# Seven channel-major products take both halves of x in one pass of 512 columns

## The chip, the cores and the metric

One core of a Trainium2 chip runs the whole kernel. The metric is the device time of one execution in microseconds, taken as the median of several runs. The engines work side by side and synchronise through semaphores: PE (TensorE) multiplies matrices, PEld is its weight load, DVE (VectorE) and ACT (ScalarE) do elementwise work and read PSUM, POOL (GpSimd) does a little, SP (SyncE) issues the DMAs.

## The reference

Two transformer-like blocks follow each other on 256 tokens of 1024 channels, all in float32.

```python
# block 1: S5 state-space branch and dilated attention
h = rms_norm(x, norm_w)
u_s, z_s, q, k, v, z_a, r_s, r_a = split(h @ w_in)
y_s = (s5_branch(u_s, ..., w_glu) * silu(z_s)) @ w_ssm_out     # s5: g * sigmoid(g @ w_glu)
y_a = (dilated_attention(q, k, v) * silu(z_a)) @ w_attn_out
x = x + (sigmoid(r_s) * y_s + sigmoid(r_a) * y_a) @ w_o
# block 2: HGRN2 branch, differential attention, mixture of experts
h = rms_norm_2(x, norm_mix)
hq, hf, hi, hog, dq, dk, dv, gate_hg, gate_da = split(h @ w_in_2)
o_hg = rms_norm_2(hgrn2(hq, 1 - f, hi, log(f))) * silu(hog)    # f from hf
mixed = sigmoid(gate_hg) * (o_hg @ w_branch_hg) + sigmoid(gate_da) * (o_da @ w_branch_da)
x = x + mixed @ w_out
x = x + hier_moe(rms_norm_2(x), ...)                           # top 2 of 8 experts in 1 of 4 groups
```

## The kernel before

**Products in three terms.** A float32 product is done in PE's fp32r format with both operands split into a rounded part (hi) and a remainder (lo). Each product is w_hi·x_hi + w_hi·x_lo + w_lo·x_hi, summed in PSUM. Weights arrive by DMA as float32 half-blocks of 128 partitions by 1024 values (512 KB) in buffers WR2 or WR3. ACT copies such a half-block to an fp32r buffer (the hi part, a copy of 128x1024 at line 272), DVE subtracts that from the original (the lo part, 128x1024 at line 253). Five fp32r buffers (one called WR0, two WR1, two WR4) rotate through these hi and lo parts. So the lo part of a half-block goes to the buffer that PE gives back when it ends the half-block two before it, and is needed when PE ends the one before it.

**The function `dense`** (line 438) computes 256 output channels by 256 tokens in one PSUM bank, called d (there are two of them). It takes two half-blocks of weights, one for each half of the 1024 input channels. Each half-block is 2 groups of 128 channels (j) by 4 slices of input channels (kk) by three terms: 24 matmuls of 256 columns at line 453, 48 for the block. Then `evac` reads the bank: DVE or ACT takes both j in one instruction of 128x512.

**What runs.** Block 1 ends with the gate rs (4 blocks), the product glu (4), the attention output ao (4, with smaller weights), the state-space output so (4) and the output product wo. Block 2 begins with hf and hq (2 blocks), then hi, hog (2), dq, dk, dv, the gates gh (4) and gd (4), the branch outputs bh and bd, and the last product wo2. hi, dq, dk, dv, wo and wo2 are token-major: `dense_wide` (line 467), matmuls of 512 columns at line 477, with other halves of the weights. `dense2` (line 489) does hf at line 502. The sequential parts (dilated attention, HGRN2, differential attention) are generators that give side work to PE between half-blocks (`side_run`); lines 935, 954 and 969 are the dilated attention's matmuls.

**Order.** The program's order is what the code issues, after a scheduler that moves an instruction of an engine ahead of others where it reckons that these would wait; each engine then runs its own list strictly in order. `prefetch` issues the loads of the mixture's weights at a rate per block, as far as there is free space. The mixture (lines 1995 and 2027) ends the kernel.

**PSUM.** Its eight banks are d (2 tiles of one bank), s (3 tiles of one bank), s2 (one tile of two banks) and o (one bank). s2 is used by the scan of HGRN2 and by a few steps of the first block. A tile has its readers and writers tracked as a whole where parts of it cannot be told apart.

Of the kernel before, what the change touches and what calls it, by code (L numbers as in the profile page):

```python
# [205 lines left out]
class Buf:  # L206
# [7 lines left out]
    def free(self):  # L214
        h = self.heap
        h.clock += 1
        for i in range(self.s, self.s + self.nu):
            assert h.used[i]
            h.used[i] = False
            h.freed[i] = h.clock  # L220


# [18 lines left out]
class Kernel:  # L241
# [196 lines left out]
    def dense(self, key, x_hi, x_lo, evac, token_major=False, k=8, rows_first=False):  # L438
# [26 lines left out]
        self.side_run()  # L465

    def dense_wide(self, key, x_hi, x_lo, evac):

# [124 lines left out]
    def tanh_half(self, out, ps):  # L593
        self.scaled(out, ps)
        self.act(out, out, AF.Tanh, scale=0.5)

# [436 lines left out]
    def setup(self):  # L1033
        nc, I = self.nc, self.I
        self.side, self.mid = [], []
        self.mheaps = [self.F]
# [18 lines left out]
    def first_block(self):  # L1055
# [132 lines left out]
        big = {n: F.alloc(3072, top=True) for n in "kqv"}  # L1188
        self.g_hi, self.g_lo = R.alloc(8, 256), R.alloc(8, 256)
        ssm = self.ssm(u2, u3)  # L1190
# [43 lines left out]
        def last(which, c):  # L1234

            if which == WHOLE[-1] and c == 5:
                hT.extend((R.alloc(8, 256), R.alloc(8, 256)))
                self.mid.extend(halves(i) for i in range(4))
# [5 lines left out]
        for which in ORDER[1:ORDER.index("so")]:  # L1244
# [24 lines left out]
            elif which in width:  # L1269
                g = gate[which] = F.alloc(width[which], 256)  # L1270
                for c in range(width[which] // 2):
                    self.dense(which, hT[0], hT[1], (silu2 if which[0] == "z" else tanh_half)(g, c))
# [38 lines left out]
            elif which == "glu":  # L1311
                zs = gate["zs"]
                s_hi, s_lo = R.alloc(8, 256), R.alloc(8, 256)
# [12 lines left out]
                self.g_hi.free()  # L1326
# [6 lines left out]
        for c in range(4):  # L1333
            def ev(ps, c=c):
                w = slice(2 * c, 2 * c + 2)
                self.stt(rs[:, w], rs[:, w], 1.0, ps, ALU.add, ALU.mult)
                t = self.E.alloc(2, 256)
                nat = t.ap.rearrange("p b (c s) -> p b s c", s=4)
                for b in range(2):
                    self.stt(nat[:, b], ra[:, 2 * c + b].rearrange("p (s c) -> p s c", s=4), 4.0,  # L1340
                             rs[:, 2 * c + b].rearrange("p (s c) -> p s c", s=4), ALU.mult, ALU.add)
# [6 lines left out]
        self.hT2 = R.alloc(8, 256), R.alloc(8, 256)  # L1348

# [272 lines left out]
    def second_block(self):  # L1622
# [44 lines left out]
        for c in range(2):  # L1667
            def ev(ps, c=c):
                self.scaled(hq[:, 2 * c:2 * c + 2], ps)
            self.dense("hq", hT[0], hT[1], ev)  # L1670
        hv = F.alloc(2, 512)
# [9 lines left out]
        for c in range(2):  # L1681
            def ev(ps, c=c):
                self.silu2(hog[:, 2 * c:2 * c + 2], ps)
            self.dense("hog", hT[0], hT[1], ev)
        self.side_add(hg, SIDE[3])
# [26 lines left out]
        for key in ("gh", "gd"):  # L1712
            gates[key] = F.alloc(8, 256)
            for c in range(4):
                def ev(ps, c=c, g=gates[key]):
                    self.tanh_half(g[:, 2 * c:2 * c + 2], ps)
                self.dense(key, hT[0], hT[1], ev)
        self.side_drain(hg)
        for b in hT + (self.rows,):
            b.free()  # L1720
# [525 lines left out]
def lay(inputs):  # L2246
# [22 lines left out]
    for name, blocks in (("w_in", (8, 10, 12, 20, 22, 24)), ("w_wo", (0, 2)), ("w_in_2", (4, 8, 10, 12)), ("w_wo2", (0,))):  # L2269
        for c in blocks:  # L2270
            two = A[name][c:c + 2]
            A[name][c:c + 2] = two.transpose(1, 2, 0, 3).reshape(two.shape)
    for name, key in (("w1", "w1_2"), ("w3", "w3_2"), ("w2", "w2_2")):
        w = f[key][0]
# [57 lines left out]
```

## Time and profile before

| | |
|---|---|
| median of 3 runs | 1035.3 us (1034.04 to 1035.33) |
| the profiled execution | 1034.89 us, of which the span from first to last instruction is 1033.1 us |
| mean granted TensorE clock | 0.975 |
| busy: PE, PEld, DVE, ACT | 926.3, 640.1, 518.6, 346.8 us |
| the chain that ended last, by engine | PE 53%, DMA 39%, DVE 6% |

The span is shown in 40 slices of 25.8 us on the page. Up to about slice 24 PE is busy nearly all the time, and from there the DMA engines are.

### The profile page before, as it was taken

The numbers are of one execution on the slowest core, as the hardware profiler recorded it, in microseconds if no ns is written. First come the engines' busy times: TensorE is split into PE (matmuls) and PEld (weight loads), VectorE is DVE, ScalarE is ACT, GpSimd is POOL, SyncE is SP. The second block draws the span as 40 slices with busy tenths as digits, with TensorE's granted clock in tenths as the row PEclk, the third lists the DMA queues.
The fourth block names the chain that finished last, engine by engine and source line by source line (L and its number), as shares of the span: only waits on it lengthen the run. The fifth ranks groups of instructions, "written<-read, shape, count | busy, mean of one in ns | idle before, by whom it ended". The sixth has DMA issues, their size and how long they took to land.

```text
span 1033.1 us, 17476 instructions
## 1 busy us (share of the span) xinstructions
PE 926.3 (90%) x7171; PEld 640.1 (62%) x7171; DVE 518.6 (50%) x1166; ACT 346.8 (34%) x574; POOL 13.4 (1%) x41
## 2 busy tenths in 40 slices
PE   8999999999999999999999999877868687787865
PEld 6887788998999988888999844321313122131312
DVE  8988987987767768596767521110101010010101
ACT  3227567455554457544644311000000000000000
POOL 2100000000000000000000000000000000000000
PEclk9999999999999999998999999998999998998989
DMA  7965655654437755652569899999999999999996
GB/s 258 223 192 170 173 159 163 191 185 164 160 128 238 238 197 172 194 182 87 182 200 331 339 394 419 421 423 420 421 421 421 421 422 421 421 420 423 421 417 264
DMA packets 65814, 296.91 MB, mean 287 GB/s; under 512 B 12224, under 2 KB 17728, under 8 KB 42176
## 3 DMA queue, kind: packets, MB, share of 16 engines
q1 hardware_dynamic: 65728, 295.73, 76.8%
q8 instruction: 58, 0.95, 0.4%
q14 instruction: 28, 0.23, 0.1%
HBM read 293.61 MB, written 2.10 MB: 286 GB/s over the span
## 4 chain that ended last, share of the span: by engine, by line
PE 53%; DMA 39%; DVE 6%; ACT 1%; issue 1%; SPq 0%; DVEq 0%; ACTq 0%
PE d L453 27%; DMA heap<-in_w_dram 25%; PE d L477 12%; DMA WR<-in_w_dram 12%; DVE heap L253 3%; DMA WR<-in_w_last_dram 2%; DVE WR L253 2%; PE h L1995 2%; PE s L935 1%; PE d L502 1%; ACT heap L272 1%; PE o L969 1%; PE s L954 1%; PE d L1817 1%; PE r L2027 1%
## 5 line engine op out<-in xcount | busy, mean ns | idle before, releaser
L453 PE MATMUL d<-R,WR 128*128 128x256 f32 x1920 | 240.3, 285 | 0.5 <-DVE WR L253 0.4
L453 PEld LDWEIGHTS d<-R,WR 128*128 128x128 f32 x1920 | 232.8, 192 | 5.5 <-issue 2.8
L1995 PE MATMUL h<-heap 128*32 128x512 f32 x1024 | 176.5, 667 | 61.8 <-DMA heap<-in_w_dram 60.7
L253 DVE TENSOR_TENSOR WR<-WR,WR 128x1024 fp32r<-128x1024 f32 x140 | 170.9, 1222 | 75.8 <-PE d L453 23.3
L272 ACT ACTIVATE WR<-WR 128x1024 fp32r<-128x1024 f32 x140 | 148.1, 1058 | 125.5 <-PE d L453 82.7
L1995 PEld LDWEIGHTS h<-heap 128*32 128x32 f32 x1024 | 40.0, 119 | 183.5 <-DMA heap<-in_w_dram 111.5
L477 PE MATMUL d<-WR,R 128*128 128x512 f32 x624 | 150.5, 398 | 2.9 <-ACT heap L272 1.5
L477 PEld LDWEIGHTS d<-WR,R 128*128 128x128 f32 x624 | 116.9, 190 | 29.5 <-DVE WR L253 2.2
L253 DVE TENSOR_TENSOR heap<-heap 128x512 f32<-128x512 f32 (+7 forms) x250 | 108.5, 483 | 1.8 <-PE s L785 0.7
L2027 PE MATMUL r<-WR,heap 128*32 128x512 f32 (+1 forms) x288 | 78.7, 550 | 10.3 <-DMA WR<-in_w_dram 9.3
L272 ACT ACTIVATE heap<-heap 128x512 f32<-128x512 f32 (+7 forms) x125 | 65.8, 539 | 65.2 <-DVE heap L253 29.3
L269 DVE SCALAR_TENSOR_TENSOR WR<-r,ring,WR 128x512 fp32r<-128x512 f32 (+1 forms) x18 | 12.4, 691 | 136.5 <-ACT WR L272 136.5
L2027 PE MATMUL r<-R,heap 128*32 128x512 f32 (+1 forms) x288 | 69.7, 551 | 9.4 <-ACT heap L272 4.8
L453 PE MATMUL d<-WR,WR 128*128 128x256 f32 x320 | 71.5, 382 | 2.2 <-DMA WR<-in_w_in_dram 2.2
L453 PEld LDWEIGHTS d<-WR,WR 128*128 128x128 f32 x320 | 60.1, 190 | 12.7 <-ACT R L272 3.7
L253 DVE TENSOR_TENSOR heap<-heap,h 128x512 f32<-128x512 f32 x8 | 5.5, 688 | 122.1 <-PE h L1995 122.0
L2027 PEld LDWEIGHTS r<-WR,heap 128*32 128x32 f32 x288 | 19.3, 109 | 56.7 <-DMA WR<-in_w_dram 26.8
L272 ACT ACTIVATE WR<-r,ring 128x512 fp32r<-128x512 f32 (+1 forms) x18 | 11.5, 640 | 125.0 <-PE r L2027 113.3
L272 ACT ACTIVATE heap<-h,ring 128x512 f32<-128x512 f32 x8 | 5.5, 687 | 134.5 <-PE h L1995 112.9
L269 DVE SCALAR_TENSOR_TENSOR heap<-heap,h 128x512 f32<-128x512 f32 x8 | 5.5, 688 | 83.5 <-ACT heap L272 83.4
L2027 PEld LDWEIGHTS r<-R,heap 128*32 128x32 f32 x288 | 14.8, 109 | 36.5 <-issue 15.5
L272 ACT ACTIVATE heap<-r 128x512 f32<-128x512 f32 x8 | 4.8, 597 | 80.3 <-PE r L2010 80.3
(215 smaller groups left out, 798.8 us busy)
## 6 DMA issues: line engine op xcount, KB each, us to landing
heap<-in_w_dram SPq DMA_DIRECT2D x128, 1024.0 KB, 19.8
WR<-in_w_in_dram SPq DMA_DIRECT2D x114, 512.0 KB, 3.8
R<-in_w_dram SPq DMA_DIRECT2D x28, 1024.0 KB, 19.8
WR<-in_w_dram SPq DMA_DIRECT2D x28, 1024.0 KB, 19.8
WR<-in_w_wo_dram SPq DMA_DIRECT2D x16, 512.0 KB, 5.6
WR<-in_w_glu_dram SPq DMA_DIRECT2D x8, 512.0 KB, 3.7
WR<-in_w_so_dram SPq DMA_DIRECT2D x8, 512.0 KB, 4.7
R<-in_w_last_dram SPq DMA_DIRECT2D x8, 512.0 KB, 12.6
```

Of the source, the lines that this page charges most:

```text
L253: (eng or self.V).tensor_tensor(out=out, in0=a, in1=b, op=op)
L269: self.V.scalar_tensor_tensor(out=out, in0=a, scalar=s, in1=b, op0=op0, op1=op1)
L272: self.A.activation(out, a, func, **kw)
L453: self.PE.matmul(ps[:, j], lhsT, rhs, start=h == 0 and i == 0 and n == 0, stop=h == k - 4 and kk == 3 and n == len(terms) - 1, skip_group_ ...
L477: self.PE.matmul(ps[tb], x[:, h + kk, sl], w[:, kk], start=h == 0 and kk == 0 and n == 0, stop=h == 6 and kk == 1 and n == 2)
L502: self.PE.matmul(ps[c][:, j], lhsT, rhs, start=h == 0 and i == 0 and n == 0, stop=h == 4 and kk == 3 and n == 2, skip_group_check=True)
L935: PE.matmul(ps[hh][:, cols], qT[r, q, qs], kT[r, q, k], start=True, stop=True)
L954: PE.transpose(pt[:, kb], s[:, kb * 128:(kb + 1) * 128], self.ident)
L969: PE.matmul(po[hp][r, qb], v[:, tb, g * 8 + hp * 2 + hh], ts_[hh][:, kb], start=kb == 0, stop=kb == 3)
L1817: PE.matmul(ps, x[:, 4 * h + kk, tb * 128:tb * 128 + 128], ws[h][w][:, kk], start=h == 0 and kk == 0 and n == 0, stop=h == 1 and kk == 3 a ...
L1995: PE.matmul(ph[sl[g]], xg[:, kk, sl[g]], w(name, kk // 4, g)[:, kk % 4], start=kk == 0, stop=kk == 7)
L2027: PE.matmul(pys[c][sl[g]], hT[:, kk, sl[g]], rhs, start=kk == 0, stop=kk == 3)
```

## The change

`dense_both` takes the place of `dense` for the seven products rs, glu, so, hq, hog, gh and gd: 24 blocks of 256 channels. x_hi and x_lo now lie beside each other in one buffer (R has two buffers of twice the size in place of four). The weights of these products are laid out on the host so that a half-block holds one j (128 channels) with all eight slices of input channels. For each slice one matmul of 512 columns takes w_hi against both halves of x, into the two halves of one PSUM bank, and one of 256 columns adds w_lo·x_hi to the first half: 16 matmuls per half-block in place of 24. At eviction ACT copies the second half of the bank to SBUF and DVE adds the first half (`total`), and what `evac` did on 128x512 it does on 128x256, once for each j. `turn` starts as True and is inverted before each block: the first block of a product takes its two banks as two tiles d, the second as the one tile s2, and so on in turn. Twelve of the 24 blocks take s2.

```diff
+    def dense_both(self, key, x_hi, x_lo, evac):
+        both = x_hi.both
+        self.turn = not self.turn
+        two = self.psum("s2", 2, 2, 256) if self.turn else None
+        for j in range(2):
+            ps = self.psum("d", 2, 256) if two is None else two[:, j]
+            hi, lo = self.next_weights(key)
+            w_hi, w_lo = (shaped(b.ap.rearrange("p a b -> p (a b)"), (8, 128)) for b in (hi, lo))
+            for kk in range(8):
+                self.PE.matmul(ps, w_hi[:, kk], both[:, :, kk], start=kk == 0, stop=False, skip_group_check=True)
+                self.PE.matmul(ps[:, 0], w_lo[:, kk], both[:, 0, kk], start=False, stop=kk == 7, skip_group_check=True)
+                if kk % 4 == 3:
+                    self.run_mid(1)
+            hi.free()
+            lo.free()
+            self.advance()
+            if j:
+                self.prefetch()
+            evac(ps, j)
+            self.side_run()
+
+    def total(self, out, ps):
+
+        self.act(out, ps[:, 1], AF.Copy)
+        self.add(out, out, ps[:, 0])
...
+    def tanh_half_both(self, out, ps):
+        self.total(out, ps)
+        self.mul(out, out, self.rows.ap)
         self.act(out, out, AF.Tanh, scale=0.5)
...
-            self.R = Slots(self.keepp, "R", (8,) * 4, (F32R,) * 4)
+            self.R = Slots(self.keepp, "R", (16,) * 2, (F32R,) * 2)
...
                 for c in range(4):
-                    def ev(ps, c=c):
-                        w = slice(2 * c, 2 * c + 2)
-                        t, y = self.E.alloc(2, 256), self.E.alloc(2, 256)
-                        self.act(t.ap, ps, AF.Tanh, scale=0.25)
+                    def ev(ps, j, c=c):
+                        w = 2 * c + j
+                        t, y = self.E.alloc(256), self.E.alloc(256)
+                        self.total(t.ap, ps)
+                        self.act(t.ap, t.ap, AF.Tanh, scale=0.25)
...
-                    self.dense("glu", self.g_hi, self.g_lo, ev)
+                    self.dense_both("glu", self.g_hi, self.g_lo, ev)
...
-            def ev(ps, c=c):
-                w = slice(2 * c, 2 * c + 2)
-                self.stt(rs[:, w], rs[:, w], 1.0, ps, ALU.add, ALU.mult)
-                t = self.E.alloc(2, 256)
...
+            def ev(ps, j, c=c):
+                w = 2 * c + j
+                t = self.E.alloc(256)
+                self.total(t.ap, ps)
+                self.stt(rs[:, w], rs[:, w], 1.0, t.ap, ALU.add, ALU.mult)
...
-            self.dense("so", s_hi, s_lo, ev)
+            self.dense_both("so", s_hi, s_lo, ev)
...
+BOTH = ("rs", "glu", "so", "hq", "hog", "gh", "gd")
```

The first place is PE in the second block of so, before: d_3666 is the block's bank, R2 and R3 are x_hi and x_lo, and row by row the half-block WR0 with WR1 gives way to the half-block WR1 with WR4.

```order
L453 MATMUL d_3666<-R2_61,WR1_911 128x256
L453 MATMUL d_3666<-R2_61,WR0_910 128x256
L453 MATMUL d_3666<-R3_62,WR0_910 128x256
L453 MATMUL d_3666<-R2_61,WR1_911 128x256
L453 MATMUL d_3666<-R2_61,WR1_911 128x256 [waits Activation_49]
L453 MATMUL d_3666<-R3_62,WR1_911 128x256
L453 MATMUL d_3666<-R2_61,WR4_67 128x256 [waits DVE_49]
L453 MATMUL d_3666<-R2_61,WR1_911 128x256
```

Here one half-block follows the other directly, and the waits are those for the weights' hi part (ACT) and lo part (DVE). The same place in the change: s2_3596 is the two-bank tile of so's second block, d_3647 the first bank of the third block.

```order
L497 MATMUL s2_3596<-R1_60,WR0_908 128x512
L498 MATMUL s2_3596<-R1_60,WR1_909 128x256
L497 MATMUL d_3647<-R1_60,WR4_65 128x512 [waits DVE_49,Activation_49]
L498 MATMUL d_3647<-R1_60,WR0_908 128x256 [waits DVE_49]
L497 MATMUL d_3647<-R1_60,WR4_65 128x512
L498 MATMUL d_3647<-R1_60,WR0_908 128x256
L497 MATMUL d_3647<-R1_60,WR4_65 128x512
L498 MATMUL d_3647<-R1_60,WR0_908 128x256
L497 MATMUL s2_3596<-R1_60,WR1_909 128x512 [waits DVE_49]
L498 MATMUL s2_3596<-R1_60,WR4_65 128x256
L497 MATMUL s2_3596<-R1_60,WR1_909 128x512
```

Between the two halves of s2_3596 stand six matmuls of the next block, and the first matmul of the second half waits for DVE. The second place is DVE at the same moment. Before, WR rows are lo parts of weights, the row from d_3606 is the eviction of so's first block, the strided 128x4x64 rows and the R row belong to it:

```order
L253 TENSOR_TENSOR WR4_67<-WR3_110,WR1_911 128x1024 [waits DVE_49,DMAHW3_49,PE_49,Activation_49]
L269 SCALAR_TENSOR_TENSOR heap_58<-heap_58,d_3606 128x512 [waits PE_49]
L269 SCALAR_TENSOR_TENSOR heap_58<-heap_58 128x4x64 [waits DVE_49]
L269 SCALAR_TENSOR_TENSOR heap_58<-heap_58 128x4x64
L253 TENSOR_TENSOR WR0_910<-WR3_110,WR4_67 128x1024 [waits DMAHW4_49,PE_49,Activation_49]
L253 TENSOR_TENSOR R0_59<-heap_58,R1_60 128x512 [waits Activation_49]
```

In the change, where WR0 with WR4 is the half-block that d_3647 takes:

```order
L272 TENSOR_TENSOR heap_58<-heap_58,d_3570 128x256 [waits Activation_49]
L288 SCALAR_TENSOR_TENSOR heap_58<-heap_58 128x256 [waits DVE_49]
L288 SCALAR_TENSOR_TENSOR heap_58<-heap_58 128x4x64 [waits DVE_49]
L272 TENSOR_TENSOR WR0_908<-WR3_108,WR4_65 128x1024 [waits DMAHW4_49,PE_49,Activation_49]
L272 TENSOR_TENSOR R0_59<-heap_58,R0_59 128x256 [waits Activation_49]
L272 TENSOR_TENSOR heap_58<-heap_58,s2_3596 128x256 [waits Activation_49]
L288 SCALAR_TENSOR_TENSOR heap_58<-heap_58 128x256 [waits DVE_49]
```

The add that empties the first half of s2_3596 (the row from s2_3596) now stands behind the lo part of the next block's weights, which takes over the buffer WR0 that this half of s2_3596 uses. The third place is PE in the last block of glu, in the change (before, its two half-blocks read like those of so above): s2_3364 is its tile, WR4 with WR0 the first half-block, WR1 with WR1 the second.

```order
L498 MATMUL s2_3364<-R0_59,WR0_908 128x256
L497 MATMUL s2_3364<-R0_59,WR4_65 128x512
L498 MATMUL s2_3364<-R0_59,WR0_908 128x256
L497 MATMUL s2_3364<-R0_59,WR1_909 128x512 [waits DVE_49]
L498 MATMUL s2_3364<-R0_59,WR1_909 128x256
```

Here nothing of other work stands between the halves. On DVE the order at this place is:

```order
L272 TENSOR_TENSOR WR4_65<-WR3_108,WR4_65 128x1024 [waits DMAHW2_49,PE_49]
L272 TENSOR_TENSOR R1_60<-heap_58,R1_60 128x256 [waits Activation_49]
L272 TENSOR_TENSOR heap_58<-heap_58,s2_3364 128x256 [waits Activation_49]
L288 SCALAR_TENSOR_TENSOR heap_58<-heap_58 128x256 [waits Activation_49]
L272 TENSOR_TENSOR heap_58<-heap_58 128x256 [waits DVE_49]
```

Again the add from s2_3364 stands behind a lo part of weights, that of ao's first half-block, and behind one row of an earlier split.

## Rows read from the trace of the kernel before

**Rows 1.** The page's 40 slices: busy tenths, granted clock, DMA.
```profile
PE 8999999999999999999999999877868687787865
...
PEclk9999999999999999998999999998999998998989
DMA  7965655654437755652569899999999999999996
```

**Rows 2.** Waits of PE, 391 to 426 us: who for whom, us, times, longest.
```profile
PE d L477 <- DVE WR L253: 1.0, 1, 1.0
```

**Rows 3.** Busy time of each engine in seven stretches.
```profile
core 0: us, PE busy (x) PEld busy (x) DVE busy (x) ACT busy (x) POOL busy (x), PEclk, DMA share, GB/s
255.60:289.70 34.10, 34.10 (x301) 32.16 (x301) 23.66 (x67) 18.68 (x32) 0.00 (x0) 1.00 0.44 148
289.70:331.00 41.30, 41.21 (x360) 39.66 (x359) 30.70 (x45) 22.53 (x33) 1.09 (x2) 1.00 0.58 191
331.00:355.00 24.00, 24.00 (x201) 23.98 (x200) 17.14 (x22) 10.07 (x12) 0.00 (x0) 1.00 0.71 223
...
476.50:538.00 61.50, 61.42 (x482) 56.36 (x480) 44.95 (x116) 35.01 (x73) 0.00 (x0) 1.00 0.51 171
538.00:561.00 23.00, 23.00 (x192) 22.87 (x191) 18.13 (x23) 10.36 (x12) 0.00 (x0) 1.00 0.89 321
561.00:597.00 36.00, 35.31 (x219) 29.96 (x217) 22.58 (x68) 13.65 (x28) 3.36 (x15) 1.00 0.91 337
597.00:623.00 26.00, 25.48 (x221) 11.46 (x224) 4.97 (x19) 3.67 (x10) 0.00 (x0) 1.00 0.96 394
623.00:1033.00 410.00, 315.05 (x1774) 106.06 (x1766) 41.93 (x118) 29.32 (x56) 0.00 (x0) 0.95 0.99 411
```

**Rows 4.** Chain that ended last, 240 to 640 us: start us, us, what.
```profile
261.65 1.02 PE o L969 x16
...
414.67 11.51 PE d L453 x96
426.19 21.87 PE d L477 x96
...
561.07 11.01 PE d L477 x48
...
623.69 19.82 DMA heap<-in_w_dram
```

**Rows 5.** Timeline of DVE: start us, us, operation; around 253 and 330 us.
```profile
253.39 0.68 DVE L253 TENSOR_TENSOR heap<-d,heap 128x512 f32<-128x512 f32 x1
253.99 0.42 DVE L253 TENSOR_TENSOR heap<-o,heap 128x256 f32<-128x256 f32 x1
...
329.01 1.23 DVE L253 TENSOR_TENSOR WR<-WR,WR 128x1024 fp32r<-128x1024 f32 x1 [1.38 <-issue]
330.15 0.68 DVE L269 SCALAR_TENSOR_TENSOR heap<-heap,d 128x512 f32<-128x512 f32 x1
331.89 1.23 DVE L253 TENSOR_TENSOR WR<-WR,WR 128x1024 fp32r<-128x1024 f32 x1 [1.06 <-issue]
```

**Rows 6.** Timeline of ACT at 495 us.
```profile
495.04 1.06 ACT L272 ACTIVATE WR<-WR 128x1024 fp32r<-128x1024 f32 x1
496.01 0.36 ACT L272 ACTIVATE heap<-s 128x256 f32<-128x256 f32 x1
```

**Rows 7.** Groups by line and shape, DVE, 255 to 538 us: busy us, mean ns.
```profile
L253 DVE TENSOR_TENSOR heap<-d,heap 128x512 f32<-128x512 f32 x18 | 12.3, 683 | 0.2 <-ACT heap L272 0.2
L253 DVE TENSOR_TENSOR R<-heap,R 128x512 fp32r<-128x512 f32 x10 | 6.9, 689 | 3.6 <-ACT R L272 3.6
...
L269 DVE SCALAR_TENSOR_TENSOR ring<-ring 128x8 f32<-128x8 f32 x22 | 3.6, 166 | 0.7
...
L253 DVE TENSOR_TENSOR heap<-heap 128x256 f32<-128x256 f32 x8 | 3.0, 420 | 0.0
```

More of the change, by code (lines that the diff above doesn't have):

```diff
@@ L220, in free, with __init__, __getitem__, halves_of @@
             h.freed[i] = h.clock
+class Side:
+    def __init__(self, both, i):
+        self.both, self.i, self.ap = both, i, both[:, i]
+    def __getitem__(self, key):
+        return self.ap[key]
+    def free(self):
+        if self.i:
+            self.both.free()
+def halves_of(heap, *shape):
+    both = heap.alloc(2, *shape)
+    return Side(both, 0), Side(both, 1)
 def shaped(ap, shape):
@@ L594, in tanh_half, with silu2_both @@
         self.scaled(out, ps)
+        self.act(out, out, AF.Tanh, scale=0.5)
+    def silu2_both(self, out, ps):
+        t = self.E.alloc(256)
+        self.total(t.ap, ps)
+        self.mul(out, t.ap, self.rows.ap)
+        self.act(t.ap, out, AF.Tanh, scale=0.5)
+        self.stt(out, t.ap, 1.0, out, ALU.add, ALU.mult)
+        t.free()
+    def tanh_half_both(self, out, ps):
+        self.total(out, ps)
+        self.mul(out, out, self.rows.ap)
         self.act(out, out, AF.Tanh, scale=0.5)
@@ L1270, in first_block @@
                 g = gate[which] = F.alloc(width[which], 256)
-                for c in range(width[which] // 2):
+                for c in range(width[which] // 2 if which in BOTH else 0):
+                    self.dense_both(which, *hT, lambda ps, j, c=c, g=g: self.tanh_half_both(g[:, 2 * c + j], ps))
+                for c in range(0 if which in BOTH else width[which] // 2):
                     self.dense(which, hT[0], hT[1], (silu2 if which[0] == "z" else tanh_half)(g, c))
@@ L1333, in first_block @@
         for c in range(4):
-            def ev(ps, c=c):
-                w = slice(2 * c, 2 * c + 2)
-                self.stt(rs[:, w], rs[:, w], 1.0, ps, ALU.add, ALU.mult)
-                t = self.E.alloc(2, 256)
[L1338 to L1341, printed above, removed]
+            def ev(ps, j, c=c):
+                w = 2 * c + j
+                t = self.E.alloc(256)
+                self.total(t.ap, ps)
+                self.stt(rs[:, w], rs[:, w], 1.0, t.ap, ALU.add, ALU.mult)
+                self.stt(t.ap.rearrange("p (c s) -> p s c", s=4), ra[:, w].rearrange("p (s c) -> p s c", s=4), 4.0,
+                         rs[:, w].rearrange("p (s c) -> p s c", s=4), ALU.mult, ALU.add)
                 self.split(m_hi[:, w], m_lo[:, w], t.ap)
                 t.free()
-            self.dense("so", s_hi, s_lo, ev)
+            self.dense_both("so", s_hi, s_lo, ev)
         for b in (s_hi, s_lo, ra, rs):
@@ L1667, in second_block, with ev @@
         for c in range(2):
-            def ev(ps, c=c):
-                self.scaled(hq[:, 2 * c:2 * c + 2], ps)
-            self.dense("hq", hT[0], hT[1], ev)
+            def ev(ps, j, c=c):
+                self.total(hq[:, 2 * c + j], ps)
+                self.mul(hq[:, 2 * c + j], hq[:, 2 * c + j], self.rows.ap)
+            self.dense_both("hq", hT[0], hT[1], ev)
         hv = F.alloc(2, 512)
@@ L1714, in second_block, with ev @@
             for c in range(4):
-                def ev(ps, c=c, g=gates[key]):
-                    self.tanh_half(g[:, 2 * c:2 * c + 2], ps)
-                self.dense(key, hT[0], hT[1], ev)
+                def ev(ps, j, c=c, g=gates[key]):
+                    self.tanh_half_both(g[:, 2 * c + j], ps)
+                self.dense_both(key, hT[0], hT[1], ev)
         self.side_drain(hg)
-        for b in hT + (self.rows,):
+        for b in (*hT, self.rows):
             b.free()
@@ L2272, in lay @@
             A[name][c:c + 2] = two.transpose(1, 2, 0, 3).reshape(two.shape)
+    for name, blocks in (("w_in", range(28, 32)), ("w_glu", range(4)), ("w_so", range(4)),
+                         ("w_in_2", (0, 1, 6, 7, *range(14, 22)))):
+        for c in blocks:
+            A[name][c] = A[name][c].reshape(128, 8, 2, 128).transpose(0, 2, 1, 3).reshape(128, 8, 256)
     for name, key in (("w1", "w1_2"), ("w3", "w3_2"), ("w2", "w2_2")):
```

16 lines of the change are left out of this document (8 added, 8 removed).

## Prediction

> **What bounds the kernel now.** I read the slices first, then the waits of PE by stretch, then the busy time by stretch. The slices show PE at nine tenths up to slice 24 and DMA at nine tenths from there to the end [rows 1]. The waits of PE in the part that changes come to one of 1.0 us, for a weight's lo part where hi begins [rows 2]; from 255 to 391 and from 476 to 561 us there is none. So PE is the bound there: busy 34.10 of 34.10, 24.00 of 24.00 and 61.42 of 61.50 us in stretches with rs, so, and gh with gd [rows 3], at a granted clock of 1.00. DVE is the second engine: 0.69, 0.74, 0.71 and 0.73 of the time in the first four of these stretches. From 623.69 us the chain is loads of the mixture's weights, with DMA at 0.99 [rows 3, 4]. These loads are issued a few per block of PE's work as space comes free, so I take PE's time before 597 us to pass on to the end one for one. DMA is idle 0.11 x 23 + 0.09 x 36 + 0.04 x 26 = 6.8 us between 538 and 623 us [rows 3]; were none of that tied to PE, a delay of up to 6.8 us could vanish in it. I keep that for a rival.
>
> **The gain on PE.** 24 blocks of 2 halves of 8 slices are 384 times one matmul of 512 columns in place of two of 256. Matmuls of 256 took 11.51 / 96 = 119.9 ns, those of 512 21.87 / 96 = 227.8 and 11.01 / 48 = 229.4 ns [rows 4]; with 228.6, one saves 239.8 - 228.6 = 11.2 ns, 384 save 4.3 us. The new matmul reads x with a step between its two halves, which no row shows: if that broke its stream in two, the gain would be nothing; by the better of the two rows it is 12.0 x 384 = 4.6 us. I take 4.3. Four in six weight loads remain and hide as before.
>
> In these rows a matmul takes about 13 ns more than its columns at full clock (119.9 - 106.7). The Trainium skill (TensorE: Matmul & The Clock Gate, section Back-to-back issue gap) states about 2.5 ns for an isolated one, and warns there that weight loads add to it in a real stream. By its 2.5 ns the gain would be only an estimated 384 x 2.5 = 1.0 us, and the sum below +8.4; the trace has the larger figure, so the rows stand.
>
> **The cost at eviction, where it is covered.** An eviction of 128x512 takes 0.68 us on DVE, one of 128x256 0.42 [rows 5, 7]. A gate block (rs, gh, gd) or an hq block had one multiply of 0.68 and now has two adds and two multiplies, 1.68: +1.0 us on DVE, 14 times. so has +1.0 a block, glu +1.5 (its four operations become ten of half the size, 4.2 for 2.7), hog +1.2 (two become six). Together 14 + 4 + 6 + 2.4 = 26 us of DVE, and about as many ACT copies of 0.36 [rows 6] as there are halves, 48 x 0.36 = 17 us. While DVE keeps up this lies beside PE's work and costs nothing. With it DVE is busy 36.7 of 41.3 us with glu, 21.1 of 24.0 with so, 53.0 of 61.5 with gh and gd: under 0.9, but with little left, so a late lo part or add is not made up quickly.
>
> **The cost that isn't covered.** Twelve blocks use the two-bank tile. There the first matmul of the second half waits for DVE's add that empties the first half (in one block for ACT's copy), as the order shows for so and glu. Call E the moment PE ends the first half. In all twelve, DVE's queue has the lo part of the next half-block's weights ahead of that add, and this lo part goes to the buffer that PE gives back at E. So DVE starts it at E, the next instruction 1.14 us later (329.01 to 330.15 [rows 5]), the add takes 0.42: the second half starts at E + 1.6, plus whatever else stands between. ACT's copy (0.36) runs beside the lo part. In the meantime PE does what the scheduler put between: it is free only of the difference. I price this work by its rows: 0.23 a matmul of 512, 0.12 of 256, 0.064 of 128 (1.02 / 16 [rows 4]).
>
> - rs: 1.15 and 1.5 us of other work, waits 0.5 and 0.1.
> - glu: 1.03 us of other work, wait 0.6; then none, and an R row (0.36 to 0.42) ahead of the add: 2.0.
> - so: the six matmuls of the next block are 1.04 us, but three of them need that lo part, done at E + 1.22; they end at E + 1.22 + 0.12 + 2 x 0.35 = E + 2.0, wait 1.0. Then eight wide ones, 1.83 us: 0.1.
> - hq and hog: eight or so wide ones, 1.8 us, against E + 2.0 with a multiply ahead of the add: 0.2 each.
> - gh: 1.98 us against E + 2.8 (two R rows of 128x512, 0.6 each), wait 0.8; 0.78 against 1.75, with an instruction of 128x8 or smaller (0.17 [rows 7]) ahead of the add: 1.0.
> - gd: 0.94 against 1.6, wait 0.7; 0.72 against 1.75, again with a small one: 1.0.
>
> That is 0.6 + 2.6 + 1.1 + 0.4 + 1.8 + 1.7 = 8.2 us. It supposes DVE free at E. At 0.85 busy it is sometimes in an instruction; 0.1 us a place, 1.2 us, is an estimate for that, from a rest of 0.2 to 0.5 us of an instruction of 0.42 to 1.23 that is met in a third of the places. Bounds: where half of the shorter waits are hidden and only the four of 1 us or more stand, 5.0; where DVE comes half an instruction of 1.23 late everywhere, 8.2 + 12 x 0.6 = 15.4. Nothing here can give a gain.
>
> The trace before has nothing of this: one half-block follows another on PE, and its lo part starts at the end of the half two before (329.01, then 331.89, a half-block apart [rows 5]), 1.2 us of work in a half of 2.9. The Trainium skill (PSUM — Partial Sum Buffer, section Summary: rules for kernel authors) says to read PSUM beside a running matmul from a different bank. The two halves of the tile are in different banks, so by that rule the wait need not be, and the sum would be the gain alone; it is the program's semaphore that asks for it, and no run here shows it yet.
>
> **Sum.** -4.3 + 8.2 + 1.2 = +5.1 us. From the profiled execution's 1034.9 (span 1033.1 and 1.8 around it) that is 1040.0, and from the median of the runs, 0.4 above it, 1040.4. The other edits cost nothing that I can find: DMA sizes are the same, the layout of R takes the same space, and the few moves on SP are under loads that are early by half-blocks.
>
> **Rivals.**
> 1. *The gain alone.* The waits are hidden: PE's fillers reach to the add, the add is not late. Then 1035.3 - 4.3 = 1031.0. For it: PE was the bound, a scheduler chose the fillers, and DVE's shares stay under 0.9. Against it: glu's last block has no filler, and in no other does the work between reach the add. It decides where the waits fall under 2.2 us in all, a quarter of my sum.
> 2. *Nothing to be seen.* The waits come to some 5 us, near their lower bound, against 4.3 of gain, or a delay is taken up in the 6.8 us of DMA idle before 623 us. 1035.3 to 1036.5. For it: that idle time exists. Against it: loads are issued by PE's blocks.
> 3. *DVE becomes the bound.* The added 26 us push it over where it is at 0.86 to 0.89, so that lo parts come late in blocks without s2 too. At one lo part of 1.23 us late in half of the 12 other blocks, 7.4 us come on top: 1047.8. Against it: the averages still leave 4.6 us with glu and 8.5 with gh and gd.
>
> **How the numbers follow.** The forecast, waits of 6 to 13 us, has 0.66; rival 1 0.10, rival 2 0.14, rival 3 0.10. A change of over 0.2% (2.1 us) is about what the measurement can tell from none. Faster is rival 1, 0.10; same is rival 2 with part of the forecast's lower end, 0.16; slower the rest, 0.74. The forecast's own range is 1036.5 to 1045; with the rivals, 1033 to 1046 leaves out about 0.1 at each end.
>
> **What would show it.** In the profile of the changed kernel, waits of matmuls at line 497 on DVE's add at twelve places, 8 to 10 us in all, the longest (2 us) in glu's last block. 96 pairs of a stretch without waits at 347 to 349 ns each, not 359. The stretch of so (331 to 355 us [rows 3]) is 24.0 us before, and I expect 64 x 0.0112 = 0.7 less and 1.1 more: 24.4. The mixture's loads from the first of 19.8 us to the end keep their length. It would be wrong if these waits are under 4 us, or if the end moves by less than half of what PE loses before 597 us.

## The result, and the profile after

The changed kernel takes 1043.39 us (median of 6 runs, 1040.73 to 1044.26) against 1034.24 us before (median of 6). The forecast was +5.1 us (1040.4 us, range 1033 to 1046). By these two medians the change is 9.1 us slower; the ratio on record, with its 95% interval, is 1.0074 (1.0063 to 1.0085), which is 6.5 to 8.8 us slower and 7.7 in the middle. Against the median of 21 further executions of the kernel before (1035.19 us, timed with the experiments below) it is 8.2 us, and a second timing of the change gave 1.0061, 6.3 us. So the change is slower by 6 to 9 us; the texts below use the ratios. The profiled execution is the fastest of the six, 1040.73 us with a span of 1039.0, which is 5.9 us over the span before.

The page of the changed kernel, span, busy shares and the slices:

```profile
span 1039.0 us, 16832 instructions
...
PE 931.8 (90%) x6787; PEld 619.4 (60%) x6787; DVE 537.8 (52%) x1256; ACT 364.4 (35%) x648; POOL 13.4 (1%) x41
...
PE   8999999999999999999999999877878687786875
...
DMA  7965645654436664653559899999999999999996
```

The picture is the same as in [rows 1], PE first and DMA from slice 24 on. DVE has 19.2 us more than the 518.6 before, ACT 17.6 more than 346.8. To see where the time went, a few marks of the chain of waits (start us, us, what) are laid side by side: attention's matmuls before rs's first block, hf's last 48, the 89 to 96 wide matmuls of dq, the 16 behind HGRN2, wo2, and the mixture. Before, beside the rows in [rows 4]:

```profile
252.27 1.02 PE o L969 x16
...
381.88 5.76 PE d L502 x48
...
474.15 1.68 PE s L1477 x16
...
604.32 10.44 PE h L1995 x96
```

After, in the profiled execution:

```profile
252.08 1.02 PE o L1029 x16
...
387.14 5.77 PE d L549 x48
...
433.63 20.23 PE d L524 x89
...
478.30 1.68 PE s L1539 x16
...
566.96 11.01 PE d L524 x48
...
610.00 10.44 PE h L2058 x96
...
629.29 19.81 DMA heap<-in_w_dram
```

A second profiled execution of the same kernel, taken later, with the same columns:

```profile
252.88 1.02 PE o L1029 x16
...
386.79 5.77 PE d L549 x48
...
433.26 20.18 PE d L524 x89
...
479.40 1.68 PE s L1539 x16
...
568.04 11.00 PE d L524 x48
...
611.51 10.44 PE h L2058 x96
```

The differences of these marks give the time of each part (us; the second column ends where dq's wide matmuls end, start plus duration; "PE idle" is the length less PE's busy time, summed over the three parts that hold the change, the first, second and fourth; "span" is the profiled execution's). The rows from the fourth on are kernels of the experiments below:

| kernel | rs, glu, ao, so, wo | hf, hq, hi, hog, dq | HGRN2 and dv | gh, gd, bh, bd | wo2 | rest | PE idle | span |
|---|---|---|---|---|---|---|---|---|
| before | 129.61 | 66.18 | 26.09 | 86.92 | 43.25 | 428.8 | 1.2 | 1033.1 |
| after | 135.06 | 66.72 | 24.44 | 88.66 | 43.04 | 429.0 | 6.3 | 1039.0 |
| after, second profile | 133.91 | 66.65 | 25.96 | 88.64 | 43.47 | 429.1 | 6.4 | 1040.6 |
| all blocks in d | 129.51 | 65.84 | 26.03 | 86.44 | 43.04 | 428.9 | 2.3 | 1032.6 |
| the same, 512 as 2 x 256 | 130.75 | 66.24 | 27.56 | 87.56 | 43.19 | 429.0 | 2.3 | 1036.2 |
| all in d, two blocks in s | 129.15 | 64.83 | 24.57 | 86.39 | 43.03 | 428.9 | 0.6 | 1029.5 |
| the same, wide first | 129.20 | 64.49 | 27.52 | 85.68 | 43.39 | 429.0 | 1.4 | 1031.2 |
| after, wide first | 130.80 | 65.70 | 26.04 | 86.66 | 43.64 | 428.9 | 3.2 | 1033.4 |

From wo2 on the parts are the same to 0.7 us: PE's loss passes to the end. Against the kernel before, two parts hold it, the first and the one with gh and gd. HGRN2's part has no block of the change in it and differs by up to 3 us from one profile to the next.

The waits of PE between 240 and 640 us (who for whom, us, times, longest), the five longest:

```profile
PE s L497 <- DVE heap L272: 1.9, 1, 1.9
PE d L498 <- DVE WR L272: 1.6, 2, 1.0
PE d L524 <- DVE WR L272: 1.1, 2, 0.7
PE d L472 <- DVE WR L272: 1.0, 1, 1.0
PE d L524 <- DVE heap L272: 0.6, 1, 0.6
```

Before there was one of 1.0 in the parts that change [rows 2]. The first of the five is at glu's last block, whose two halves follow each other on PE without other work. PE's timeline there in the first profile (start us, us, operation, idle time before it and what ended it):

```profile
316.50 0.28 PE L498 MATMUL s<-R,WR 128*128 128x256 f32 x1
318.65 0.50 PE L497 MATMUL s<-R,WR 128*128 128x512 f32 x1 [1.87 <-DVE heap L272]
318.99 0.27 PE L498 MATMUL s<-R,WR 128*128 128x256 f32 x1
319.10 0.40 PE L497 MATMUL s<-R,WR 128*128 128x512 f32 x1
...
320.09 0.63 PE L497 MATMUL s<-R,WR 128*128 128x512 f32 x1
320.52 0.41 PE L498 MATMUL s<-R,WR 128*128 128x256 f32 x1
```

DVE at the same moment:

```profile
316.70 1.23 DVE L272 TENSOR_TENSOR WR<-WR,WR 128x1024 fp32r<-128x1024 f32 x1 [0.43 <-PE s L497]
317.85 0.42 DVE L272 TENSOR_TENSOR R<-heap,R 128x256 fp32r<-128x256 f32 x1
318.18 0.41 DVE L272 TENSOR_TENSOR heap<-heap,s 128x256 f32<-128x256 f32 x1
```

The lo part of ao's weights starts as PE ends the last wide matmul of the first half, the add that empties it comes third, and PE goes on 1.87 us after it stopped. ACT's copy ran beside the lo part (316.88, 0.38 us). So the wait is what the prediction's queue made it, 2.0 worked out and 1.87 measured.

What it did not have is in the last two rows of PE: pairs that took 0.35 us take 0.64. The windows show the clock there (PE, PEld, DVE, ACT and POOL busy, granted clock, DMA share and GB/s):

```profile
316.70:318.65 1.95, 0.08 (x1) 0.00 (x1) 1.89 (x3) 1.37 (x4) 0.00 (x0) 1.00 0.75 267
319.45:322.65 3.20, 3.20 (x12) 2.71 (x11) 1.45 (x5) 1.71 (x5) 0.00 (x0) 0.50 0.68 248
```

PE ran on at full clock for 0.8 us after the gap, and then the clock was at 0.50, 1.2 of 2.4 GHz, for 3.2 us: half of that, 1.6 us, went. In the second profile PE had the same gap of 1.87 us and no fall:

```profile
317.66:319.60 1.94, 0.13 (x2) 0.00 (x0) 1.89 (x3) 1.35 (x3) 0.00 (x0) 1.00 0.83 291
320.40:323.60 3.20, 3.20 (x23) 2.92 (x21) 2.34 (x6) 2.40 (x7) 0.00 (x0) 1.00 0.68 239
```

This accounts for 135.06 against 133.91 in the first part, to 0.5 us. A third profile has the same gap, that of the change with only gh and gd in d (an experiment below, with nothing altered up to here), and there the fall is back:

```profile
319.80 0.50 PE L497 MATMUL s<-R,WR 128*128 128x512 f32 x1 [1.87 <-DVE heap L272]
...
321.30:324.50 3.20, 3.20 (x13) 2.82 (x12) 1.71 (x4) 1.22 (x5) 0.00 (x0) 0.50 0.59 234
```

So the fall came in two of three profiles with this gap. In the other ten profiles of this document the clock from 313 to 331 us is 1.00.

In HGRN2's part the clock falls too, in the kernel before as well, and more in one execution than in the next: from 450 to 480 us it was 0.94 in the first profile and 0.89 in the second and in the kernel before. HGRN2's part is 1.5 us longer in the second profile than in the first, the first part 1.15 shorter, and the start of the first mark (0.8) and wo2 (0.4) add the rest: so one profile gives +5.9 us and the other +7.5.

In so, the six matmuls of the next block that stand in the gap end late, as forecast: the first narrow one waits 1.03 us for its lo part (DVE's 343.77, 1.22 us), and the second half starts 345.97 - 343.62 = 2.35 us after the first ended, where the prediction had 2.0.

```profile
343.62 0.40 PE L497 MATMUL d<-R,WR 128*128 128x512 f32 x1
345.05 0.39 PE L498 MATMUL d<-R,WR 128*128 128x256 f32 x1 [1.03 <-DVE WR L272]
...
345.97 0.40 PE L497 MATMUL s<-R,WR 128*128 128x512 f32 x1
```

Followed through the twelve places in this way, PE stands idle behind a first half at six of them: 1.87 us in glu, 1.03 and 0.66 in so, 0.62 and 0.40 in hq, 0.55 in gh and 1.01 in gd, 6.1 us in all. Only the 1.87 us is a wait for the add that empties s2. The 0.62 is a matmul of hi whose tile d waits for the eviction of hq's first block (DVE's add at 405.31, behind a scan of 2.29 us), and the other 3.65 us are work, pulled forward into the gap, that waits for its own lo part. The kernel before has 1.0 us at hi as well [rows 2]. At the other six places (two in rs, one each in glu, hog, gh and gd) no idle time is seen.

### The profile page after: what moved, and what is told of

Its sections match the earlier page's. It is cut to its first block, busy times and chain, and to the rows that moved or that the text cites. A ratio compares the mean times of both kernels' runs of the same rounds, so it can differ in the third digit from the quotient of the medians.

```text
span 1039.0 us, 16832 instructions
## 1 busy us (share of the span) xinstructions
PE 931.8 (90%) x6787; PEld 619.4 (60%) x6787; DVE 537.8 (52%) x1256; ACT 364.4 (35%) x648; POOL 13.4 (1%) x41
## 4 chain that ended last, share of the span: by engine, by line
PE 50%; DMA 38%; DVE 8%; ACT 2%; issue 1%; SPq 0%; DVEq 0%; ACTq 0%
DMA heap<-in_w_dram 25%; PE d L472 13%; PE d L524 12%; DMA WR<-in_w_dram 12%; PE s L497 4%; PE d L497 4%; DVE heap L272 3%; DVE WR L272 3%; PE h L2058 2%; PE d L498 2%; PE s L498 2%; ACT heap L291 1%; PE s L995 1%; DMA WR<-in_w_last_dram 1%; PE d L549 1%
## 5 line engine op out<-in xcount | busy, mean ns | idle before, releaser
L2058 PE MATMUL h<-heap 128*32 128x512 f32 x1024 | 182.3, 691 | 57.8 <-DMA heap<-in_w_dram 56.9
L272 DVE TENSOR_TENSOR heap<-heap 128x512 f32<-128x512 f32 (+7 forms) x286 | 122.1, 468 | 2.3 <-PE s L845 0.7
L472 PE MATMUL d<-R,WR 128*128 128x256 f32 x768 | 96.4, 285 | 1.5 <-DVE WR L272 1.4
L291 ACT ACTIVATE heap<-heap 128x256 f32<-128x256 f32 (+5 forms) x147 | 72.1, 500 | 72.7 <-DVE heap L272 37.1
L472 PEld LDWEIGHTS d<-R,WR 128*128 128x128 f32 x768 | 93.3, 192 | 3.2 <-DVE WR L272 2.1
L497 PE MATMUL s<-R,WR 128*128 128x512 f32 x192 | 71.9, 413 | 1.9 <-DVE heap L272 1.9
L497 PE MATMUL d<-R,WR 128*128 128x512 f32 x192 | 69.9, 403 | 0.0
L498 PE MATMUL d<-R,WR 128*128 128x256 f32 x192 | 54.5, 284 | 1.6 <-DVE WR L272 1.6
L498 PE MATMUL s<-R,WR 128*128 128x256 f32 x192 | 54.5, 284 | 0.0
```

The lines of the kernel that those rows point to most:

```text
L272: (eng or self.V).tensor_tensor(out=out, in0=a, in1=b, op=op)
L291: self.A.activation(out, a, func, **kw)
L472: self.PE.matmul(ps[:, j], lhsT, rhs, start=h == 0 and i == 0 and n == 0, stop=h == k - 4 and kk == 3 and n == len(terms) - 1, skip_group_ ...
L497: self.PE.matmul(ps, w_hi[:, kk], both[:, :, kk], start=kk == 0, stop=False, skip_group_check=True)
L498: self.PE.matmul(ps[:, 0], w_lo[:, kk], both[:, 0, kk], start=False, stop=kk == 7, skip_group_check=True)
L2058: PE.matmul(ph[sl[g]], xg[:, kk, sl[g]], w(name, kk // 4, g)[:, kk % 4], start=kk == 0, stop=kk == 7)
```

## Experiments

The theory after this: most of the loss is the wait between the two halves of the twelve blocks in s2, with DVE's order (lo part, then add) as its length. Rivals: DVE's added load of about 20 us costs by itself, wherever the sums stand; or the clock's fall carries the timed difference. In the cuts of code, `...` stands for lines left out.

**All blocks in d.** One line is changed:

```diff
-        two = self.psum("s2", 2, 2, 256) if self.turn else None
+        two = None
```

> All 24 blocks take two tiles d, none the two-bank tile s2; nothing else differs from the change. Theory (the loss is the wait of a block's second half for the eviction of its first, with the halves pulled forward into that gap and the fall of the clock after the longest of these waits): the second half's first matmul waits for nothing, PE's idle time in glu, so, gh and gd (1.9 + 1.7 + 1.6 us in the changed kernel's profile) goes, the granted clock stays at 1.00 between 255 and 391 us, and the gain of 384 x 6.4 ns = 2.5 us (353 for 359.4 ns a pair) is left: 1031 to 1033 us against some 1034.2 before, ratio 0.997 to 0.999. Rival (the 26 us of added eviction on DVE are the cause, wherever the sums lie): DVE has the same work, so the time stays within 2 us of the changed kernel's, 1039 to 1044, ratio 1.005 or more.

Measured: 1034.04 us, ratio 0.9983 (0.9974 to 0.9992), 1.8 us faster than before and 9.4 us faster than the change by the ratios (8.1 against the change's second timing). The waits left in 240 to 640 us, those over 0.5:

```profile
PE d L472 <- DVE heap L272: 1.2, 1, 1.2
PE d L497 <- DVE heap L272: 1.1, 1, 1.1
```

The parts with glu and with gh and gd fall to 129.51 and 86.44. DVE has the same 1256 instructions as in the change, so the tile and not the load makes this difference. The gain is 0.5 to 1 us smaller than expected, since two new waits stand there, one at ao and one at hq's second block: a tile d that PE needs is still waiting for the eviction of an earlier block (at hq behind the scan of 2.29 us on DVE).

**All blocks in s2.**

```diff
-        two = self.psum("s2", 2, 2, 256) if self.turn else None
+        two = self.psum("s2", 2, 2, 256)
```

> The dose the other way: all 24 blocks take the one two-bank tile s2. Theory: 24 places in place of 12 where a second half waits for an add, and each block's first half waits for the eviction of the block before as well, so the loss at least doubles: 1048 to 1065 us, ratio 1.014 to 1.03. Rival (DVE's load): the same instructions on DVE, so within 2 us of the changed kernel, 1039 to 1045.

Measured: 1075.65 us, ratio 1.039 (1.0374 to 1.0406), 40 us slower than before. The row of the wait for the add now reads:

```profile
PE s L497 <- DVE heap L272: 24.2, 23, 2.1
```

The direction is right and the dose beyond the range. Of the 23 waits 12 are at a block's first half and 11 at its second, ten of them 1.5 to 1.6 us long; the row holds 24 of the 40 us, and the rest was not followed up.

**512 columns as two times 256**, on the kernel with all blocks in d:

```diff
-                self.PE.matmul(ps, w_hi[:, kk], both[:, :, kk], start=kk == 0, stop=False, skip_group_check=True)
+                for i in range(2):
+                    self.PE.matmul(ps[:, i], w_hi[:, kk], both[:, i, kk], start=kk == 0 and i == 0, stop=False, skip_group_check=True)
```

> As the kernel with all blocks in tiles d, but each matmul of 512 columns is issued as two of 256 with the same weights: the three matmuls of before in the new layout. It prices the wide matmul alone. Theory from the changed kernel's trace (353 ns a pair against 3 x 119.8): 384 x 6.4 ns = 2.5 us slower than the kernel with all blocks in d, 1034 to 1036 us. By the prediction's price (348.5) 4.3 us slower. Rival (wide matmuls give nothing, a pair's pace is set by the weight loads): the same time to 0.5 us.

Measured: 1037.59 us, ratio 1.0017 (1.0006 to 1.0029), 0.0034 or 3.5 us over the kernel with 512 columns. Of that, 27.56 against 26.03 in HGRN2's part is no doing of the edit; the other parts give 1.24 + 0.40 + 1.12 = 2.8 us, 7.2 ns for each of the 384 wide matmuls. So the wide matmul has a gain, and it is 2.8 and not 4.3 us. PE's busy time in these parts says the same (2.8 us); against the kernel before, the kernel with all blocks in d has 2.0 us less.

**Other matmuls in the gap of glu's last block**, in the changed kernel:

```diff
+            elif key == "glu" and two is not None and self.glu_fill:
+                self.glu_fill -= 1
+                if self.glu_fill == 0:
+                    warm = self.psum("s", 512)
+                    for i in range(8):
+                        self.PE.matmul(warm, both[:, 0, 0, :128], both[:, :, 0], start=i == 0, stop=i == 7)
...
-        self.side, self.mid, self.turn = [], [], True
+        self.side, self.mid, self.turn, self.glu_fill = [], [], True, 2
```

> The changed kernel with eight more matmuls of 512 columns (x against x, 8 x 0.229 = 1.8 us, their result is read by nobody) between the two halves of glu's last block, in the gap of 1.9 us where PE waited. Theory (after that gap the granted clock was 0.50 for 3.2 us, which cost 1.6 us): the gap is still there for the products but PE does not idle, the clock stays at 1.00, and the end comes 1.5 to 3 us sooner than the changed kernel's, ratio to before some 1.0045 to 1.006. Rival (the slow stretch is no consequence of the gap, or costs nothing at the end): same time as the changed kernel, ratio 1.007 to 1.008.

Measured: 1041.17 us, ratio 1.0054 (1.0041 to 1.0068), inside what the theory expected. But the profile's first part is 133.80 us, as in the second profile of the change (133.91), where the clock did not fall either, and a second timing of the change (below) is 1.0061, 1.0044 to 1.0079. The intervals overlap: how much the clock costs on average over executions stays open; that it can cost 1.2 to 1.6 us in one is what the first profile shows. With the gap filled the profile has a clock of 1.00 here, but so has the second profile of the change with the gap open.

**The change once more.**

> The changed kernel once more, for a second profile beside these runs. Its profiled execution was 1040.7 us while five others lay between 1042.8 and 1044.3. Theory (the slow stretch of the clock between 450 and 480 us, in HGRN2's part, takes in more or less of the work from run to run: 0.94 in that profile, 0.89 in that of before): a profile at 1042 to 1044 us has the same waits to 0.3 us and a granted clock under 0.92 there. Rival: the waits themselves differ between runs by some us.

Measured: 1042.03 us, ratio 1.0061; the second profile above. The same waits came back to 0.3 us, and the clock between 450 and 480 us was 0.89, as expected. That the fall in glu was missing was not expected.

**DVE's load.** All blocks in d, with DVE in place of ACT for the copy, and the eviction issued ahead of the next split:

```diff
             hi.free()
             lo.free()
+            evac(ps, j)
             self.advance()
             if j:
                 self.prefetch()
-            evac(ps, j)
...
-        self.act(out, ps[:, 1], AF.Copy)
+        self.V.tensor_copy(out, ps[:, 1])
```

> All blocks in tiles d, and DVE makes the copy of the second half itself (48 copies of 128x256 on DVE in place of ACT, 48 x 0.34 to 0.42 = 16 to 20 us more on DVE); the eviction's code is also issued ahead of the next split. It is the direct test of the rival that DVE's load is what costs. Theory (DVE has room where PE doesn't wait on a shared tile): within 1.5 us of the kernel with all blocks in d, 1033 to 1036 us. Rival (DVE's load): 26 us of more DVE work cost the change 8 us, so 16 to 20 us more cost at least 4: 1038 us or more.

Measured: 1038.62 us, ratio 1.0035 (1.0025 to 1.0045), 5.4 us over the kernel with ACT's copies, which is what the rival forecast. In its profile the longest waits of matmuls for DVE are these:

```profile
PE d L524 <- DVE WR L272: 1.3, 1, 1.3
PE d L472 <- DVE WR L272: 0.9, 1, 0.9
PE d L472 <- DVE heap L272: 0.6, 1, 0.6
```

So DVE has not the room that the theory gave it. With tiles d the change's own evictions show 2.3 us of waits, the two above; 14 us more of DVE's busy time (551.6 against 537.4) cost 5.4. Most of the 5.4 does not show as waits of PE: these three rows come to 2.8 us. The order of the eviction was altered as well, so the 5.4 are for both.

**Only glu in d, only gh and gd in d.** Two kernels, the change with one condition more:

```diff
-        two = self.psum("s2", 2, 2, 256) if self.turn else None
+        two = self.psum("s2", 2, 2, 256) if self.turn and key != "glu" else None
...
+        two = self.psum("s2", 2, 2, 256) if self.turn and key not in ("gh", "gd") else None
```

> The changed kernel, but the four glu blocks take tiles d, the others as in the change (ten of 24 blocks in s2). Theory by the profile of the change: the gap of 1.9 us in glu's last block and the 1.6 us of slow clock behind it go, a wait of some 1.2 us of ao for the later eviction of that block comes (it stands in the kernel with all blocks in d), so about 2.3 us less than the changed kernel: ratio 1.0045 to 1.006. With the sums of the prediction (waits of 0.6 and 2.0 in glu) 2.6 less, without any clock. Rival (the wait counts only where it is visible as idle time of PE, and the clock costs nothing): 0.7 us less, ratio 1.0065 or more.

Measured: 1040.43 us, ratio 1.0052 (1.0038 to 1.0066). The first part falls from 133.91 to 132.25, 1.7 us. The wait of 1.9 goes and one of 1.2 comes at ao; PE's idle time falls by 1.0 us and its busy time by 0.7. Against the second timing of the change (1.0061) the gain in time is within the intervals.

> The changed kernel, but gh and gd take tiles d (eight of their blocks; four of these had s2). Stretch from the start of the 16 matmuls behind dv to wo2: 86.9 us before, 88.66 and 88.64 in the two profiles of the change, 86.44 with all blocks in d. Theory (waits per place): this stretch falls to 86.4 to 86.7 and the others stay, so 2.1 us less than the changed kernel, ratio 1.004 to 1.0055. Rival (DVE's load in this stretch, 0.86 busy, is what costs there): the stretch stays over 88 us.

Measured: 1039.72 us, ratio 1.0043 (1.0029 to 1.0057). The part of gh and gd runs from 481.88 to 568.16, 86.28 us, 2.4 less than in the change, as expected, while DVE does the same work in it. The first part, 134.82 us, has the fall of the clock shown above.

**All in d, with two blocks in the tiles s**, so that nothing waits for these evictions (block 7 is glu's last, block 12 hq's first):

```diff
-        two = self.psum("s2", 2, 2, 256) if self.turn else None
+        two = None
+        self.count = getattr(self, "count", -1) + 1
+        kind = "s" if self.count in (7, 12) else "d"
...
-            ps = self.psum("d", 2, 256) if two is None else two[:, j]
+            ps = self.psum(kind, 2, 256)
```

> As the kernel with all blocks in d, but glu's last block and hq's first take two of the three one-bank tiles s, so that ao's first and hq's first matmuls need not wait for an eviction (1.2 and 1.1 us of PE's idle time in that kernel's profile, both put down to DVE). Theory: these 2.3 us go and nothing else waits: 1031 to 1032.5 us, ratio 0.9955 to 0.998. Rival (behind the wait for the tile stands the lo part of the weights, due at the same moment): under 0.5 us of gain, ratio 0.998 to 0.999.

Measured: 1033.23 us, ratio 0.9978 (0.9968 to 0.9988). Both waits are gone from its profile (in the parts that change the largest of a matmul for DVE is 0.3 us), and the parts are 0.36 and 1.0 us shorter. By ratio the gain over the kernel with all in d is 0.5 us and within the intervals.

**Wide matmuls first**, on that kernel and on the changed kernel with its s2:

```diff
             for kk in range(8):
                 self.PE.matmul(ps, w_hi[:, kk], both[:, :, kk], start=kk == 0, stop=False, skip_group_check=True)
+                if kk == 7:
+                    self.run_mid(1)
+            for kk in range(8):
                 self.PE.matmul(ps[:, 0], w_lo[:, kk], both[:, 0, kk], start=False, stop=kk == 7, skip_group_check=True)
-                if kk % 4 == 3:
+                if kk == 7:
                     self.run_mid(1)
```

> The kernel with d tiles and two blocks in s, but in each half the eight matmuls of 512 columns come first and then the eight of 256, so that the lo part of the weights is needed 1.8 us later. Theory A (in alternation a pair costs 353 ns, 4.5 ns over the 348.6 of the two kinds by themselves): up to 384 x 4.5 ns = 1.7 us faster than that kernel, 1031 to 1032.5 us, ratio 0.9955 to 0.997. Theory B (the pair's pace does not hang on the order; the 353 are what these operands take): within 0.5 us of it, ratio 0.9973 to 0.9983. The small waits for lo parts (0.3 us) go in both.

Measured: 1032.93 us, ratio 0.9975 (0.9963 to 0.9987). hog's 32 pairs, no wait between them, in its profile:

```profile
412.47 1.98 PE L499 MATMUL d<-R,WR 128*128 128x512 f32 x8
...
423.61 4.74 PE L529 MATMUL d<-WR,R 128*128 128x512 f32 x20
```

That is 11.14 / 32 = 348.1 ns a pair. In the kernel with all in d, where the kinds alternate, hog's first wide matmul starts at 414.76 and its last, the 32nd, at 425.70: 10.94 / 31 = 352.9 ns. Theory A holds for the pace, but its range of times is missed and B's met: the 1.8 us that this pace gives in 384 pairs stand against a new wait of 1.4 us at ao for DVE and a longer HGRN2 part (27.52 us), so that the time is not told apart from the kernel above.

> The changed kernel with s2 as it is, and in each half the eight wide matmuls first, then the eight narrow ones. It takes apart what the blocks in s2 wait for. The waits for the lo part of the work pulled forward (1.0 us in so, put down to DVE's lo part) go or shrink, since only wide matmuls stand in the gap; those for the add stay. Theory (both halves of the loss hang on the add, and the lo part only hides behind it): about the changed kernel's time less 0.5 to 1.5 us, ratio 1.005 to 1.007, and the wait of so is put down to the add. Rival (the lo part is the cause): most of the loss goes, ratio under 1.003.

Measured: 1036.39 us, ratio 1.0008 (0.9999 to 1.0018). This is the rival's result: with s2 as it is, the time is nearly that of the kernel before. The profile shows how. glu's last block on PE:

```profile
314.76 1.11 PE L501 MATMUL s<-R,WR 128*128 128x256 f32 x8
316.90 2.14 PE L497 MATMUL s<-R,WR 128*128 128x512 f32 x8 [1.03 <-DVE heap L272]
```

and on DVE:

```profile
314.96 1.23 DVE L272 TENSOR_TENSOR WR<-WR,WR 128x1024 fp32r<-128x1024 f32 x1
316.10 0.42 DVE L272 TENSOR_TENSOR R<-heap,R 128x256 fp32r<-128x256 f32 x1
316.44 0.41 DVE L272 TENSOR_TENSOR heap<-heap,s 128x256 f32<-128x256 f32 x1
```

The hi buffer is given back after the last wide matmul, 0.95 us before the half ends, so the lo part that takes it over starts that much sooner and the add behind it too: the gap is 1.03 in place of 1.87 us. In so, where wide matmuls alone stand in the gap, the wait of 1.03 us is gone. In hq little changes: 0.45 and 0.41 in place of 0.62 and 0.40. The wait in glu needs both: the shared tile makes PE wait for the add, and the lo part ahead of it, 1.14 of the 1.6 us, makes it long.

Not all of this gain is the wait's. The new order also has the faster pace of the run before it, so the cost of s2 in this order is the difference from that run: 1.0008 against 0.9975, 3.4 us, or 1.6 + 1.2 + 1.0 = 3.8 us in the three parts. In the alternating order s2 costs 8.8 us in the same parts (the second profile of the change against the kernel with two blocks in s: 4.8 + 1.8 + 2.2). So by one profile of each kernel the order takes off 5.0 us, somewhat more than half of what s2 costs, and 3.8 us stay.

## Why the prediction was right

**The mechanism held, though its own sign did not show.** PE was the bound and its loss passed to the end: all parts from wo2 on are equal to 0.7 us, and DMA's idle time before 623 us took up nothing (so that half of rival 2 is out). The loss is that of the blocks in s2, and it goes when the tile goes (all blocks in d, ratio 0.9983). But the prediction named waits of line 497 on the add at twelve places, 8 to 10 us in all, and called itself wrong if they came to under 4 us. Read by the letter that is what happened: there is one such wait, of 1.87 us. What it described for so alone, work in the gap that waits for its own lo part, is the commoner form, and half of the places show no idle time.

**The sum of the waits came out, and partly by luck.** From the second profile and the table, the parts with the change lost (133.91 - 129.61) + (66.65 - 66.18) + (88.64 - 86.92) = 6.5 us. With the 2.8 us that the wide matmuls gave, s2 cost 9.3 us; the prediction had 8.2 + 1.2 = 9.4. The direct comparison, with the kernel with all in d and two blocks in s, has 8.8. Of these 8.8 PE's idle time is 5.8 (6.4 less 0.6) and 3.0 lie in its busy time; for the first part the rows are these, the change's second profile first:

```profile
252.88:386.79 133.91, 130.09 (x838) 110.91 (x839) 104.83 (x214) 78.72 (x145) 1.09 (x2) 1.00 0.57 187
...
252.68:381.83 129.15, 128.63 (x838) 110.42 (x839) 104.28 (x214) 78.26 (x145) 1.09 (x2) 1.00 0.60 194
```

Which instructions hold the 3.0 us stays open. By place the prediction missed both ways, and the misses cancel. gh and gd took 1.7 + 0.9 (128 pairs at 7.2 ns) = 2.6 us, not 3.5. hq and hog took 0.5 + 0.5 = 0.9 us, not 0.4. The first part took 4.3 + 1.4 = 5.7 us (4.8 in the direct comparison), not 4.3; 0.7 of that is the wait for the lo part of the wide matmuls pulled forward at wo, which the prediction had left out as covered.

**The term that was mis-sized is the gain on PE:** 4.3 us predicted, 2.8 measured. The prediction added the paces of two streams of one kind each [rows 4], 228.6 + 119.8 = 348.4 ns, and gave 347 to 349 ns as a sign. In alternation a pair took 352.9; grouped, 348.1. The rows were right and the sum was not, because the order of the new loop was not in them. Its rival ends, 0 and 4.6, held it. DVE's added work was sized too high as well, 26 us for 19.2: the prediction added durations, and in DVE's rows above an instruction of 0.42 us is followed by the next after 0.33. This term cost nothing in the sum. With both measured terms the sum is -2.8 + 9.3 = +6.5 us. What is left up to +7.7 is not in a profile that was kept: five of the six timed executions took 1042.8 to 1044.3 us, and only the sixth and one of the second timing (1042.34) were profiled.

**What was not foreseen.** PE's clock can fall to half behind a gap of 1.87 us; the prediction named a granted clock of 1.00 and priced a gap at its own length alone. And the range's upper rival, DVE as the bound, has more to it than the 0.10 it got: not in the change itself, but 14 us of DVE's work more, with the eviction's order altered, cost 5 us at once.

**Of the two rules of the Trainium skill** that were weighed, the one on the gap between matmuls (TensorE: Matmul & The Clock Gate, section Back-to-back issue gap) would have given an estimated 1.0 us of gain; 2.8 were measured, so neither that nor the rows alone. The one on banks (PSUM — Partial Sum Buffer, section Summary: rules for kernel authors) is borne out in the kernel with all blocks in d: halves in two tiles need not wait for each other, and the loss is gone.

A version that beats both kernels: all blocks in d with two in s, with or without the wide matmuls first, 1032.9 to 1033.2 us, ratios 0.9975 and 0.9978 to before.

## What to carry to other kernels

Where two halves of a tile are written and read in turn, give each half a tile of its own: a tile that is tracked as a whole makes the second half wait for the eviction of the first, and that wait is as long as whatever stands ahead of the eviction on its engine. Before taking the pace of two kinds of instruction from two streams, look whether the new loop alternates them. And look at what frees a buffer: here eight matmuls moved ahead of eight others gave a buffer back 0.95 us sooner, and took 5.0 of the 8.8 us off that the shared tile cost.

## What the runs showed of the hardware

A stretch of PE at 0.50, 3.2 us long, followed a gap of 1.87 us in two of three profiled executions with the same gap (1.6 us lost in the first), and not in the third, which ran the same program as the first. Alternating matmuls of 512 and of 256 columns took 352.9 ns a pair, groups of eight of each 348.1 ns; what makes the 4.8 ns was not found.
